# A transformer kernel of two blocks: the order of TensorE's instructions chosen from 80 plans, and 16 additions moved from GpSimd to VectorE

## The chip, the core and the metric

One core of a Trainium2 chip runs the kernel in one launch. The metric is the device time of one execution in microseconds (us). Three runs of the kernel before gave 2123.08, 2125.76 and 2126.22 us, median 2125.76 us.

In the profile PE is TensorE (matmuls and transposes), PEld its weight loads, ACT is ScalarE, DVE is VectorE, POOL is GpSimd and SP is SyncE, which issues the DMAs.

## What is computed

Two small transformers follow each other on one sequence of 256 tokens with 1024 channels, each two layers deep. All is fp32.

```python
def first_block(x, mem, ...):                      # two layers
        y = hybrid_mixer(x, ...)                   # three attentions, 8 heads of 64, gated and added
        x = layer_norm(alpha * x + y, ...)
        y = memory_cross_attention(x, mem, ...)    # 4 heads of 128
        x = layer_norm(alpha * x + y, ...)
        y = swiglu_ffn(x, w_gu, w_down)            # hidden width 2816
        x = layer_norm(alpha * x + y, ...)

def second_block(x, c, ...):                       # two layers
        h = _rmsnorm(x) * (1.0 + sc1) + sh1        # sc, sh, g come from c @ w_mod
        x = x + HALF_STEP * g1 * _swiglu(h, ...)
        h = _rmsnorm(x) * (1.0 + sc2) + sh2
        x = x + g2 * _hybrid_mixer(h, ...)         # stick-breaking, dilated, HGRN2; 4 heads each
        h = _rmsnorm(x) * (1.0 + sc3) + sh3
        x = x + HALF_STEP * g3 * _swiglu(h, ...)
```

In the first block's mixer the three branches are merged as `sum over n of sigmoid(gate_n) * (branch_n @ w_branch[n])`.

## The kernel before

**Tiling.** The 256 tokens are two halves of 128, and each half is a thread t = 0 or 1 with tiles of its own. A weight matrix comes in chunks of 128x1024 (tile `raw`). ScalarE rounds a chunk to fp32r (tile `wh`, or `E`), VectorE subtracts to get the rest (`wl`, or `E`), and both threads use the pair. The activations are split in the same way into two `S` tiles. A product is then three fp32r matmuls (`mm3`: high by high, low by high, high by low), each with 512 columns as a rule, added up in PSUM. A wide product gathers in `m` (one bank a thread), everything else in `a` (three banks a thread). Attention scores, the products of the probabilities with the values, and all transposes are plain fp32 matmuls of 128 columns in `a`. A plain fp32 matmul that is no transpose stands in the trace as two MATMUL records.

**Two forms of TensorE.** In `values` the heads are 64 wide, so the output has 64 partitions and the instruction uses half of the array's columns (tile size 128x64, in a row of the trace `128*64`, in the order `64x128`). Every other matmul uses the whole array (128x128). There are 192 matmuls of the first kind: 384 records. Below, a *visit* is an unbroken run of 64-wide matmuls between two whole-array instructions.

**What sets the order.** The program doesn't emit its instructions at once. A `Recorder` collects them with their tiles and dependencies, `plan` puts them in an order, and `emit` issues them in that order, all engines' queues at once. `listed` is a list scheduler. It keeps for each engine the instructions whose operands are ready by its own table of costs (`cost`), and takes the one with the earliest deadline `late`. The deadlines come from TensorE's instructions in the order in which the program recorded them: each is due when the slots before it are used up, and what it depends on is due earlier by its duration times `SLACK`. With `ROUNDS = 1` there is one plan. A change between the two forms of TensorE costs nothing in it.

**Around the moved work.** `branch` multiplies a product by its gate on VectorE and adds it to `merged` (tile `X`) on GpSimd for the second and third branch: 2 halves by 2 branches by 2 threads by 2 layers, 16 additions of 128x512. `transposed(merged, 8)` reads the sums on TensorE. `modulated` opens each of the second block's six parts in each thread, 12 times in all: two sums of squares from ScalarE are added with an epsilon by two small GpSimd instructions, a third takes the power -1/2 (`pow`), and VectorE scales `x` by it for eight transposes.

All instructions carry one line number in the profile, that of `emit`; tile names tell them apart.

Of the kernel before, what the change touches and what calls it, by code (L numbers as in the profile page):

```python
# [10 lines left out]
F32R = mybir.dt.float32r  # L11
U8 = mybir.dt.uint8
AF = mybir.ActivationFunctionType
ALU = mybir.AluOpType
# [7 lines left out]
RMS_EPS = 1e-6  # L22
# [107 lines left out]
TABLE = 1300  # L130
SLACK = 1.5
ROUNDS = 1
TRACE = 0
# [5 lines left out]
class Op:  # L139
    __slots__ = ("i", "eng", "name", "call", "args", "kw", "dur", "slot", "deps", "succ", "tiles", "set", "late", "start",  # L140
                 "wait", "ready", "nbytes")
# [6 lines left out]
class Recorder:  # L148
# [43 lines left out]
    def add(self, engine, name, args, kw):  # L192
        op = Op()
# [7 lines left out]
        for ap, write in [(a, False) for a in src] + [(a, True) for a in out]:  # L201
            n = ap.tensor.name
# [24 lines left out]
    def cost(self, op, name, out, src, kw):  # L227
        n = 1
        for step, k in list(out.ap)[1:]:
            n *= k  # L230
        wide = n
# [5 lines left out]
        if op.eng == "PE":  # L237
            return (4.7 + 0.4406 * n, 0) if src[1].dtype == F32R else ((1 if name == "transpose" else 2) * FP32, 0)
        if op.eng == "SP":
# [5 lines left out]
        if op.eng == "POOL":  # L245
            if name == "memset":
                return 200 + wide, 0
            return (400 if n == 1 else 700 + 2 * wide), 0
        acc = 83 if kw.get("accum_out") is not None else 0
# [13 lines left out]
    def plan(self):  # L263
        best, line = None, [op for op in self.ops if op.eng == "PE"]
        for op in self.ops:
            op.succ = []
        for op in self.ops:
            for d in op.deps:
                self.ops[d].succ.append(op.i)
        for _ in range(ROUNDS):  # L270
            order, time = self.listed(line)
            if best is None or time < best[1]:
                best = order, time, self.preload, [op.start for op in self.ops], {n: t.slot for n, t in self.tiles.items()}
            line = [op for op in order if op.eng == "PE"]
# [7 lines left out]
    def listed(self, line):  # L282

        import heapq
        ops = self.ops
# [13 lines left out]
        total = 0  # L299
        for op in line:  # L300
            op.late = total
            total += op.slot
        for op in reversed(ops):
# [9 lines left out]
            for j in reuse.get(op.i, ()):  # L313
                if ops[j].i > op.i and ops[j].late - dur < op.late:
                    op.late = ops[j].late - dur

        engines = ("PE", "ACT", "DVE", "POOL", "SP")
        ready = {e: [] for e in engines}
# [23 lines left out]
        dma, table, order, busy = 0.0, None, [], {e: False for e in engines}  # L342
        parked, later, progress = {}, [], 0.0

# [28 lines left out]
        while events:  # L373
# [18 lines left out]
            while again:  # L392
                again = False
                for e in engines:
                    if free[e] > now:
                        continue
                    q, held = ready[e], []
                    op = None
                    while q:
                        k = heapq.heappop(q)  # L400
                        if not room(k[2]):
                            continue
                        if e == "ACT" and k[2].set and table != k[2].set:
                            held.append(k)
                            if len(held) < 12:
                                continue
                            break
                        op = k[2]
                        break
                    if held and (op is None or held[0][0] + TABLE < op.late):  # L410
                        if op is not None:
# [21 lines left out]
                    free[e] = now + op.slot  # L433
                    push(free[e], 2, e)
                    end = now + op.dur
                    if e == "SP":
# [19 lines left out]
                    for j in op.succ:  # L456
                        s = ops[j]
                        v = (now + op.slot if e == "PE" else end) if s.eng == e != "SP" else end + NEXT[e][s.eng]
# [70 lines left out]
class Program:  # L529
# [173 lines left out]
    def modulated(self, x, sc, sh):  # L703
# [222 lines left out]
    def mixer(self, l, t, xT):  # L926
# [673 lines left out]
```

## Time and profile before

| | before |
|---|---|
| median of three runs | 2125.76 us |
| the profiled execution's own time | 2126.53 us |
| its span (first to last instruction) | 2124.5 us |
| TensorE busy | 2087.4 us (98%) |
| VectorE busy | 1567.6 us (74%) |
| ScalarE busy | 1214.4 us (57%) |
| GpSimd busy | 91.0 us (4%) |
| granted TensorE clock | 1.00 |

The chain of waits that ended last consists of TensorE nearly alone. A busy TensorE in this profile is not a TensorE at its peak: a record lasts longer than the step to the next one, since matmuls are pipelined, so the price of an instruction is read from start to start.

### The profile page before, as it was taken

Reading aid. Unit: us, or ns where it says so; the run is one execution under the profiler, and the core shown is the slowest. Engines: PE = TensorE matmul, PEld = TensorE weight load, DVE = VectorE, ACT = ScalarE, POOL = GpSimd, SP = SyncE. Lnnn points to the kernel's source line nnn. Section 1 sums busy time; section 2 is a strip of 40 time slices with the busy share of each in tenths; the row PEclk is TensorE's granted clock in tenths of the full one; section 3 lists DMA queues with packets and bytes.
Section 4 is the critical chain, followed back from the end, with each engine's and each line's share of the span. In section 5 each row is a group of like instructions: output and inputs, shape, how many; then the busy total and the mean of one; then the engine's idle time right before and its main releaser. Section 6 shows DMA issues by size and latency. Waiting matters only on the chain. (4 is left out here: it accounts for less than half of the span.)

```text
span 2124.5 us, 30068 instructions
## 1 busy us (share of the span) xinstructions
PE 2087.4 (98%) x10246; PEld 1690.9 (80%) x10246; DVE 1567.6 (74%) x3245; ACT 1214.4 (57%) x2538; POOL 91.0 (4%) x120
## 2 busy tenths in 40 slices
PE   8999999999999999999999999999999999999998
PEld 7788777888788878788878878878888887887887
DVE  5787888667888888877786678975566556997554
ACT  6977555444676755544454457764455445775442
POOL 0000200000000020000000000000000000000000
PEclk9999999999999999999999999999999999999999
DMA  7576776777767677688677652566656555256653
GB/s 265 162 251 217 245 252 218 253 253 257 250 218 256 215 253 256 214 265 267 227 243 246 234 182 96 160 189 189 192 176 188 171 187 185 71 162 204 187 185 105
DMA packets 150321, 443.20 MB, mean 209 GB/s; under 512 B 19208, under 2 KB 24344, under 8 KB 150168
## 3 DMA queue, kind: packets, MB, share of 16 engines
q1 hardware_dynamic: 150168, 441.29, 64.1%
q8 instruction: 80, 1.31, 0.2%
q14 instruction: 73, 0.60, 0.1%
HBM read 440.10 MB, written 1.12 MB: 208 GB/s over the span
## 5 line engine op out<-in xcount | busy, mean ns | idle before, releaser
L490 PE MATMUL m<-wh,S 128*128 128x512 f32 (+1 forms) x2944 | 932.0, 396 | 13.7 <-DVE S L490 4.6
L490 DVE TENSOR_TENSOR wl<-raw,wh 128x512 fp32r<-128x512 f32 (+1 forms) x982 | 652.4, 694 | 299.7 <-ACT wh L490 295.5
L490 ACT CAST wh<-raw 128x512 fp32r<-128x512 f32 (+1 forms) x982 | 563.9, 616 | 404.9 <-PE m L490 161.8
L490 PEld LDWEIGHTS m<-wh,S 128*128 128x128 f32 x2944 | 536.1, 188 | 137.4 <-DVE S L490 16.7
L490 PE MATMUL m<-wl,S 128*128 128x512 f32 (+1 forms) x1472 | 570.8, 392 | 0.0
L490 PE MATMUL m<-E,S 128*128 128x512 f32 x1308 | 346.0, 397 | 0.2
L490 PEld LDWEIGHTS m<-wl,S 128*128 128x128 f32 x1472 | 276.7, 188 | 56.8 <-issue 1.7
L490 PE MATMUL a<-wh,S 128*128 128x512 f32 x944 | 307.4, 399 | 3.8 <-ACT S L490 2.0
L490 DVE TENSOR_TENSOR E<-raw,E 128x512 fp32r<-128x512 f32 x334 | 218.5, 686 | 104.2 <-ACT E L490 84.7
L490 PEld LDWEIGHTS m<-E,S 128*128 128x128 f32 x1308 | 242.8, 188 | 53.7 <-DVE E L490 0.6
L490 ACT CAST E<-raw 128x512 fp32r<-128x512 f32 x334 | 192.8, 619 | 148.3 <-PE m L490 68.1
L490 PEld LDWEIGHTS a<-wh,S 128*128 128x128 f32 x944 | 173.2, 188 | 41.8 <-DVE S L490 3.7
L490 DVE SCALAR_TENSOR_TENSOR mr<-mr,c 128x512 f32<-128x512 f32 x288 | 192.7, 683 | 10.8 <-DMA mr<-in_w_mod 10.4
L490 PE MATMUL a<-E,S 128*128 128x512 f32 x648 | 184.7, 398 | 0.0
L490 PE MATMUL a<-wl,S 128*128 128x512 f32 x472 | 184.7, 394 | 0.0
L490 ACT CAST S<-a 128x256 fp32r<-128x256 f32 (+1 forms) x200 | 85.8, 429 | 126.2 <-PE a L490 125.0
L490 PEld LDWEIGHTS a<-E,S 128*128 128x128 f32 x648 | 119.7, 188 | 26.1 <-DVE E L490 0.6
L490 DVE TENSOR_TENSOR S<-a,S 128x256 fp32r<-128x256 f32 (+1 forms) x200 | 96.9, 490 | 46.0 <-ACT S L490 45.9
L490 PE MATMUL a<-c,T 128*128 128x128 f32 x652 | 120.8, 274 | 3.3 <-DVE T L490 2.4
L490 PEld LDWEIGHTS a<-c,T 128*128 128x128 f32 x652 | 84.7, 140 | 35.5 <-DVE T L490 6.3
L490 PEld LDWEIGHTS a<-wl,S 128*128 128x128 f32 x472 | 88.6, 188 | 19.3
L490 ACT ACTIVATE T<-m 128x256 f32<-128x256 f32 (+1 forms) x136 | 52.9, 389 | 78.8 <-PE m L490 78.4
(121 smaller groups left out, 1522.1 us busy)
## 6 DMA issues: line engine op xcount, KB each, us to landing
raw<-in_w_gu SPq DMA_DIRECT2D x264, 512.0 KB, 4.1
mr<-in_w_mod SPq DMA_DIRECT2D x288, 256.0 KB, 4.1
raw<-in_w_dn SPq DMA_DIRECT2D x132, 512.0 KB, 4.1
raw<-in_w_main SPq DMA_DIRECT2D x96, 512.0 KB, 4.1
raw<-in_w_in SPq DMA_DIRECT2D x56, 512.0 KB, 3.6
raw<-in_w_branch SPq DMA_DIRECT2D x24, 512.0 KB, 3.9
raw<-in_w_mo SPq DMA_DIRECT2D x16, 512.0 KB, 4.1
raw<-in_w_xkv SPq DMA_DIRECT2D x16, 512.0 KB, 4.2
```

The lines of the kernel that those rows point to most:

```text
L490: ins = op.call(*args, **{a: real(v, op) for a, v in op.kw.items()})
```

## The change

`plan` now computes the deadlines once and then makes 81 plans. It keeps the best by its own time. After a plan that is better it notes where TensorE waits for over 150 ns, and for each such wait the chain of instructions that led to it (`chain`). For the next trial one to eight of these chains get deadlines that are earlier by 0.5 to 9 us, or later by 1 us; a trial that is no better is undone. The table of costs changes too: `listed` charges a change of TensorE's form (`ENTER`, `LEAVE`), and it stays in the form it is in while an instruction of that form is ready and not due much later than the first one of another form (`STAY`: 12 us for the whole array, 25 us for the 64-wide form). `SLACK` goes from 1.5 to 1.7. In the kernel's arithmetic, the 16 additions go from GpSimd to VectorE, and in `modulated` one VectorE instruction takes the place of the two small GpSimd additions.

```diff
-SLACK = 1.5
-ROUNDS = 1
+STAY = 12000, 25000
+ENTER, LEAVE = 130, 250
+SLACK = 1.7
+SEARCH = 80
...
+        op.mode = 0
+        if op.eng == "PE" and src[1].dtype != F32R:
+            op.mode = 1 if out[0].ap[0][1] == 64 else 2 if src[0].ap[0][1] == 64 else 0
...
+        for n in range(SEARCH + 1):
+            order, time = self.listed()
             if best is None or time < best[1]:
...
+                chains = [(w, self.chain(op)) for w, op in waits]
...
+            else:
+                for op, b in trial.items():
+                    op.late += b
...
+            size = (500, 1500, 4000, 9000, -1000)[(seed >> 8) % 5]
+            for _ in range((1, 1, 2, 4, 8)[(seed >> 16) % 5]):
+                seed = seed * 1103515245 + 12345 & 0x7fffffff
+                for op in chains[(seed >> 8) % len(chains)][1]:
+                    trial[op] = size
+            for op, b in trial.items():
+                op.late -= b
...
+                        if e == "PE" and k[2].mode != mode:
+                            if not aside:
+                                limit = k[0] + STAY[mode > 0]
+                            elif k[0] > limit:
+                                aside.append(k)
+                                break
+                            aside.append(k)
+                            continue
...
+                    if e == "PE" and op.mode != mode:
+                        start = now + (LEAVE if mode else 0) + (ENTER if op.mode else 0)
+                        mode = op.mode
...
-        nc.gpsimd.tensor_scalar(m, ms[:, 0:1], RMS_EPS, None, op0=ALU.add)
-        nc.gpsimd.tensor_tensor(m, m, ms[:, 1:2], op=ALU.add)
+        nc.vector.tensor_scalar(m, ms[:, 0:1], ms[:, 1:2], RMS_EPS, op0=ALU.add, op1=ALU.add)
...
-                    nc.gpsimd.tensor_tensor(m, m, gs[h], op=ALU.add)
+                    nc.vector.tensor_tensor(m, m, gs[h], op=ALU.add)
```

The built programs have the same 9632 matmuls and transposes, the same ScalarE work but for 50 activation table loads instead of 46, and the same DMAs. VectorE has 28 instructions more, GpSimd 40 fewer. The 192 matmuls of the 64-wide form stand in 56 visits before (44 of four matmuls, 2 of three, 10 of one), and in 24 after (6 of four, 12 of eight, 6 of twelve).

Three places show it. The first is TensorE in layer 0, thread 1, where the 64-wide matmuls add to `a_155` the products of the probabilities `T` with the values `S`; the `m` tiles are wide products of the mixer. Before:

```order
L490 MATMUL a_155_751<-T_215_1001,S_108_494 64x128
L490 MATMUL m_213_998<-wl_885,S_6_168 128x256
L490 MATMUL m_194_948<-wh_820,S_25_234 128x424
L490 MATMUL m_213_998<-wh_907,S_9_193 128x256
L490 MATMUL a_155_751<-T_215_1001,S_108_494 64x128
L490 MATMUL m_213_998<-wh_907,S_10_202 128x256
L490 MATMUL m_194_948<-wh_820,S_26_240 128x424
L490 MATMUL m_213_998<-wl_919,S_9_193 128x256
L490 MATMUL a_155_751<-T_215_1001,S_127_604 64x128
```

After, at the same products:

```order
L558 MATMUL m_194_956<-wl_854,S_25_233 128x424
L558 MATMUL a_155_758<-T_199_954,S_108_494 64x128 x2
L558 MATMUL a_155_758<-T_199_954,S_127_598 64x128 x2
L558 MATMUL a_155_758<-T_215_1019,S_108_494 64x128 x2
L558 MATMUL a_155_758<-T_215_1019,S_127_598 64x128 x2
L558 MATMUL m_232_1081<-wh_973,S_161_777 128x512
```

The four single matmuls of `T_215`, each a visit of its own, and the four of `T_199` from further up now stand in one visit of eight.

The second place is TensorE at the end of layer 0's cross-attention. `a_711` is thread 1's attention output; ScalarE and VectorE split it into `S_755` and `S_756` for the output projection in `a_757` and `a_758`. `a_746` and `a_747` are the same projection of thread 0. Before:

```order
L490 MATMUL a_747_3642<-E_3453,S_745_3636 128x512
L490 MATMUL a_747_3642<-E_3467,S_744_3627 128x512
L490 MATMUL a_711_3625<-T_754_3633,S_738_3581 128x128
L490 MATMUL a_711_3625<-T_754_3633,S_739_3567 128x128
L490 MATMUL a_757_3704<-wh_3348,S_755_3700 128x512
L490 MATMUL a_758_3707<-wh_3348,S_755_3700 128x512
L490 MATMUL a_757_3704<-wh_3348,S_756_3709 128x512
```

After, first the end of `a_711` and the start of thread 0's projection, and then the start of thread 1's:

```order
L558 MATMUL a_711_3614<-T_754_3600,S_738_3576 128x128
L558 MATMUL a_711_3614<-T_754_3600,S_739_3552 128x128
L558 MATMUL a_746_3636<-wh_3313,S_744_3621 128x512
L558 MATMUL a_747_3638<-wh_3313,S_744_3621 128x512
L558 MATMUL a_746_3636<-wh_3313,S_745_3630 128x512
...
L558 MATMUL a_747_3638<-E_3429,S_745_3630 128x512
L558 MATMUL a_747_3638<-E_3445,S_744_3621 128x512
L558 MATMUL a_757_3689<-wh_3313,S_755_3642 128x512
L558 MATMUL a_757_3689<-wh_3313,S_756_3650 128x512
```

The 24 matmuls of thread 0's projection, which stood ahead of the last `a_711`, now stand between it and its use.

The third place is VectorE at the last additions of layer 0's third branch: `S_585` is the gated product, `X_28` the merged sum, `wl` the low parts of weights, `S_610` the low part of the transposed sum's first half. Before, when the addition is GpSimd's:

```order
L490 TENSOR_TENSOR S_585_2839<-m_601_2891,S_585_2839 128x512
L490 TENSOR_TENSOR wl_2944<-raw_2875,wh_2934 128x512 x2
L490 TENSOR_TENSOR S_610_2954<-a_608_2936,S_609_2948 128x512
L490 TENSOR_TENSOR wl_2969<-raw_2900,wh_2960 128x512 x2
L490 TENSOR_TENSOR S_613_2980<-a_611_2962,S_612_2973 128x512
```

After:

```order
L558 TENSOR_TENSOR S_585_2817<-m_601_2885,S_585_2817 128x512
L558 TENSOR_TENSOR wl_2923<-raw_2862,wh_2911 128x512
L558 TENSOR_TENSOR X_28_1269<-X_28_1269,S_585_2817 128x512
L558 TENSOR_TENSOR S_610_2935<-a_608_2921,S_609_2929 128x512
L558 TENSOR_TENSOR wl_2923<-raw_2862,wh_2911 128x512
```

The addition stands in VectorE's queue, one half-chunk of a weight behind the gated product.

## Rows read from the trace of the kernel before

**Rows 1.** Page, busy time: us, share of the span, instructions.

```profile
PE 2087.4 (98%) x10246; PEld 1690.9 (80%) x10246; DVE 1567.6 (74%) x3245; ACT 1214.4 (57%) x2538; POOL 91.0 (4%) x120
```

**Rows 2.** Timeline, PE, seven waits: start, us, instruction [idle before <-releaser].

```profile
338.20 0.73 PE L490 MATMUL a<-wh,S 128*128 128x512 f32 x2 [0.68 <-ACT S L490]
339.82 0.50 PE L490 MATMUL a<-wh,S 128*128 128x512 f32 x1 [0.88 <-DVE S L490]
354.03 0.50 PE L490 MATMUL m<-wh,S 128*128 128x512 f32 x1 [1.82 <-DVE T L490]
880.60 0.50 PE L490 MATMUL m<-wh,S 128*128 128x512 f32 x1 [1.68 <-DVE T L490]
1063.93 0.50 PE L490 MATMUL m<-wh,S 128*128 128x512 f32 x1 [0.70 <-DVE S L490]
1347.60 0.73 PE L490 MATMUL m<-wh,S 128*128 128x512 f32 x2 [0.68 <-ACT S L490]
1399.52 0.66 PE L490 MATMUL a<-c,X 128*128 128x128 f32 x4 [1.09 <-DVE X L490]
```

**Rows 3.** Timeline, PE, a visit of four 64-wide matmuls.

```profile
135.72 0.39 PE L490 MATMUL m<-wh,S 128*128 128x512 f32 x1
136.04 0.66 PE L490 MATMUL a<-T,S 128*64 128x128 f32 x8
136.63 0.50 PE L490 MATMUL m<-wh,S 128*128 128x512 f32 x1
136.97 0.40 PE L490 MATMUL m<-wl,S 128*128 128x512 f32 x1
```

**Rows 4.** Chain of waits, two pieces: start, us, what; 512-column matmuls, then whole-array fp32.

```profile
1833.94 1.17 PE m L490 x5
1835.11 0.89 PE a L490 x8
```

**Rows 5.** Timeline, PE, a visit of one matmul between 256-column ones.

```profile
90.52 0.39 PE L490 MATMUL m<-wh,S 128*128 128x256 f32 x2
90.85 0.43 PE L490 MATMUL a<-T,S 128*64 128x128 f32 x2
91.21 0.39 PE L490 MATMUL m<-wl,S 128*128 128x256 f32 x1
91.43 0.47 PE L490 MATMUL m<-wh,S 128*128 128x424 f32 x2
```

**Rows 6.** Timeline, all engines, around the addition of the third branch.

```profile
264.92 2.37 DVE L490 TENSOR_TENSOR wl<-raw,wh 128x512 fp32r<-128x512 f32 x2
265.14 1.60 POOL L490 TENSOR_TENSOR X<-X,S 128x512 f32<-128x512 f32 x1 [4.33 <-DVE S L490]
266.80 0.66 PE L490 MATMUL a<-c,X 128*128 128x128 f32 x4 [0.52 <-POOL X L490]
267.81 1.28 DVE L490 TENSOR_TENSOR wl<-raw,wh 128x512 fp32r<-128x512 f32 x2
```

**Rows 7.** Timeline, DVE and PE, layer norm of layer 1's cross-attention, then its transposes.

```profile
865.03 0.67 DVE L490 SCALAR_TENSOR_TENSOR X<-X,a 128x512 f32<-128x512 f32 x1
869.97 0.66 PE L490 MATMUL a<-c,X 128*128 128x128 f32 x4
```

**Rows 8.** Timeline, ACT and POOL, the small instructions of one `modulated`.

```profile
1397.30 0.18 ACT L490 ACTIVATION_READ_ACCUMULATOR X<-X 128x1 f32 x1
1397.90 0.58 POOL L490 TENSOR_TENSOR s<-s,c 128x1 f32<-128x1 f32 x1
```

**Rows 9.** Group by line: xcount, busy us, mean ns, idle us before.

```profile
L490 DVE TENSOR_SCALAR s<-s 128x1 f32<-128x1 f32 (+2 forms) x40 | 6.0, 153 | 0.1
```

**Rows 10.** Timeline, ACT, a table load and what follows it.

```profile
1807.47 1.28 ACT L486 ACT_TABLE_LOAD   x1
1808.77 0.63 ACT L490 ACTIVATE T<-T 128x512 f32<-128x512 f32 x1
```

**Rows 11.** A stretch: us, busy us (count) of each engine, granted clock, DMA share, GB/s.

```profile
1300.00:1400.00 100.00, 98.03 (x569) 80.35 (x570) 93.81 (x218) 70.31 (x161) 7.94 (x8) 1.00 0.43 134
```

More of the change, by code (lines that the diff above doesn't have):

```diff
@@ L139 @@
 class Op:
-    __slots__ = ("i", "eng", "name", "call", "args", "kw", "dur", "slot", "deps", "succ", "tiles", "set", "late", "start",
+    __slots__ = ("i", "eng", "name", "call", "args", "kw", "dur", "slot", "deps", "succ", "tiles", "set", "mode", "late", "boost", "start",
                  "wait", "ready", "nbytes")
@@ L247, in cost @@
                 return 200 + wide, 0
-            return (400 if n == 1 else 700 + 2 * wide), 0
+            return (600 if n < 8 else 700 + 2 * wide), 0
         acc = 83 if kw.get("accum_out") is not None else 0
@@ L263, in plan @@
     def plan(self):
-        best, line = None, [op for op in self.ops if op.eng == "PE"]
         for op in self.ops:
-            op.succ = []
+            op.succ, op.boost = [], 0.0
         for op in self.ops:
@@ L269, in plan @@
                 self.ops[d].succ.append(op.i)
-        for _ in range(ROUNDS):
-            order, time = self.listed(line)
+        self.deadlines()
+        best, seed, trial = None, 1, {}
+        for n in range(SEARCH + 1):
+            order, time = self.listed()
             if best is None or time < best[1]:
-                best = order, time, self.preload, [op.start for op in self.ops], {n: t.slot for n, t in self.tiles.items()}
-            line = [op for op in order if op.eng == "PE"]
+                best = order, time, self.preload, [op.start for op in self.ops], {k: t.slot for k, t in self.tiles.items()}
+                waits, stop = [], 0.0
+                for op in order:
+                    if op.eng == "PE":
+                        if op.start > stop + 150 and op.start > 15000:
+                            waits.append((op.start - stop, op))
+                        stop = op.start + op.slot
+                chains = [(w, self.chain(op)) for w, op in waits]
+                if TRACE:
+                    print(n, time)
+            else:
+                for op, b in trial.items():
+                    op.late += b
+            trial = {}
+            if not chains:
+                break
+            seed = seed * 1103515245 + 12345 & 0x7fffffff
+            size = (500, 1500, 4000, 9000, -1000)[(seed >> 8) % 5]
+            for _ in range((1, 1, 2, 4, 8)[(seed >> 16) % 5]):
+                seed = seed * 1103515245 + 12345 & 0x7fffffff
+                for op in chains[(seed >> 8) % len(chains)][1]:
+                    trial[op] = size
+            for op, b in trial.items():
+                op.late -= b
         self.preload = best[2]
@@ L280, in plan, with chain, deadlines @@
         return best[:2]
-    def listed(self, line):
-        import heapq
+    def chain(self, op):
+        out, until = [op], op.start - 14000
+        while op.deps:
+            op = max((self.ops[d] for d in op.deps), key=lambda d: d.start + d.dur)
+            if op.start < until:
+                break
+            out.append(op)
+        return out
+    def deadlines(self):
         ops = self.ops
@@ L299, in listed @@
         total = 0
-        for op in line:
-            op.late = total
-            total += op.slot
+        for op in ops:
+            if op.eng == "PE":
+                op.late = total
+                total += op.slot
         for op in reversed(ops):
@@ L342, in listed @@
         dma, table, order, busy = 0.0, None, [], {e: False for e in engines}
-        parked, later, progress = {}, [], 0.0
+        parked, later, progress, mode, idle = {}, [], 0.0, 0, 0.0
         def safe(s, t, taken):
@@ L407, in listed @@
                             break
+                        if e == "PE" and k[2].mode != mode:
[3 more added lines that the diff above has]
+                                aside.append(k)
+                                break
+                            aside.append(k)
+                            continue
+                        if e == "PE" and aside and k[0] > limit:
+                            aside.append(k)
+                            break
                         op = k[2]
                         break
+                    if aside:
+                        if op is None:
+                            aside.sort()
+                            op = aside.pop(0)[2]
+                        for k in aside:
+                            heapq.heappush(q, k)
                     if held and (op is None or held[0][0] + TABLE < op.late):
@@ L432, in listed @@
                             heapq.heappush(ready["SP"], (x.late, x.i, x))
-                    free[e] = now + op.slot
+                    start = now
+                    if e == "PE" and op.mode != mode:
+                        start = now + (LEAVE if mode else 0) + (ENTER if op.mode else 0)
+                        mode = op.mode
+                    free[e] = start + op.slot
+                    if e == "PE":
+                        if now > idle + 30 and op.dur > 150:
+                            free[e] += 100
+                        idle = free[e]
                     push(free[e], 2, e)
-                    end = now + op.dur
+                    end = start + op.dur
                     if e == "SP":
@@ L457, in listed @@
                         s = ops[j]
-                        v = (now + op.slot if e == "PE" else end) if s.eng == e != "SP" else end + NEXT[e][s.eng]
+                        v = (start + op.slot if e == "PE" else end) if s.eng == e != "SP" else end + NEXT[e][s.eng]
                         s.ready = max(s.ready, v)
```

7 lines of the change are left out of this document (5 added, 2 removed).

## The prediction, made before the changed kernel ran

> **What bounds the kernel now.** I read the page's busy times first. TensorE is busy for 2087.4 of 2124.5 us [rows 1]; the other engines leave a quarter of the span or more. So the time falls in two ways only: TensorE's 37.1 us of idle time shrink, or the same matmuls cost less. Next I read the waits of PE. Behind the first DMA they are short and many, on tiles that ScalarE or VectorE have just written. The long ones are in [rows 2], and in each the reader is to see what came late: the two parts of a split attention output at 338.20 and 339.82, a PSUM tile `m` whose reader is late at 354.03 and 880.60. None is a wait for a weight, so the DMA queue is not the limit. Last I read the timeline of PE from start to start, since busy time hides lost time, and there the 64-wide matmuls stand out.
>
> **Part one: fewer visits to the 64-wide form.** In [rows 3] a 512-column matmul starts at 135.72, and the second one behind the visit at 136.97: 1.25 us for two 512-column matmuls and four 64-wide ones. The next one starts 0.23 us behind a 512-column matmul where nothing is between (1.17 us for five in a run [rows 4]). Here it is 0.32 behind the one at 135.72 and 0.34 behind the one at 136.63: 0.09 and 0.11 us are lost in plain sight at the visit's two edges. 1.25 less 0.46 is 0.79 us for the visit. What would its four matmuls cost without a change of form? Eight whole-array fp32 records take 0.89 us [rows 4], 0.11 each. The two records of a 64-wide matmul lie on top of each other, so four such steps are 0.44 us. The visit itself costs 0.35 us.
>
> The small visit gives the other end. From 90.52 to 91.43 [rows 5] three 256-column matmuls (0.12 us each, half of the 0.23) and one 64-wide take 0.91 us. 0.55 us remain, 0.44 above the step of 0.11. So the price hangs on the visit and little on what is in it: 0.55 us with one matmul, 0.79 with four.
>
> The order has 56 visits before and 24 after, so 32 go. At 0.35 us that is 11.2 us, at 0.44 it is 14.1. If only the plain edges (0.09 and 0.11) went with a visit, and the rest stayed with each group of four, it would be 6.4 us. I take 11.2, since 44 of the 56 visits have the size of [rows 3].
>
> **Part two: TensorE's waits.** For each wait I counted the matmuls that the order puts between the last one that the late tile depends on and the one that waits.
> - 338.20 and 339.82, 0.68 + 0.88 us: none before, 24 now, 5.5 us of work at 0.23 for a chain that was 1.6 us late. Both go.
> - Four more waits of 0.67 to 0.68 us (at 545, 1348, 1851 and 1874 us; the second is in [rows 2]) have the form of the first. None between before; now 13, 33, 3 and 33. Together 2.7 us, of which I leave 0.2.
> - 880.60, 1.68 us: 4 before, 13 now. 354.03, 1.82 us: 2 before, 10 now, most of them short transposes of 0.11; I leave 0.9.
> - 1063.93, 0.70 us, and one of 0.36 just behind it, together 1.06: 10 before, 14 now. 1399.52, 1.09 us: 28 before, 36 now.
> - Two transposes that wait 0.52 us each for a GpSimd addition ([rows 6] and its double in layer 1): part three. With what I leave of the last three lines, 0.5 us.
>
> That is 0.68 + 0.88 + 2.7 + 1.68 + 1.82 + 1.06 + 1.09 + 1.04 = 10.95 us, of which 1.6 stay. New waits: in layer 1's cross-attention thread 0's projection now starts three transposes (0.33 us) behind its attention output, the pattern of 338.20 and 339.82 that costs 1.56 us without cover; I take 1.0. And the transposes of its layer norm now stand 13 matmuls behind the last projection matmul (eight fp32 of 0.22 and five of 0.23, 2.9 us), while the chain between took from 865.03 to 869.97 [rows 7], 4.9 us. A wait of about 1.1 us lies in between anyhow, and VectorE did other work in that time, so I take 0.5 (0 to 0.9). Net: 10.95 - 1.6 - 1.5 = 7.8 us.
>
> The same counts show what the change can't reach: the waits at 235, 763, 867, 1074 and 1792 us keep their distance and stay.
>
> **Part three: GpSimd's work on VectorE.** Sixteen additions at 0.64 us (half of the pair at 267.81) look like 10 us more for VectorE. [Rows 6] shows otherwise: the two weight casts at 264.92 take 2.37 us beside GpSimd's addition of 1.60, the two at 267.81 take 1.28. The addition holds VectorE up for 1.09 us, longer than doing it would. Ten of the sixteen stretch a cast like that, so about 11 us of stretch go and 10 us of work come: VectorE's load stays where it was. The chain gets shorter: 1.60 us become 0.64 ahead of the transposes that waited 0.52 us, though 13 matmuls stand there now instead of 17. What hides an addition on VectorE is its place: it waits for its own engine alone, and the half chunk of `wl` behind it is wanted microseconds later. Without that cover it costs its 0.64 us, at all sixteen 10 us.
>
> In `modulated` the second sum of squares is there at 1397.48 and `pow` starts at 1397.90 [rows 8]. These 0.42 us become one VectorE instruction of 0.15 [rows 9] and the hops to and from it: a gain of 0.2 us when VectorE is free, a loss of up to 0.5 when it has just begun a cast of 0.64. TensorE waits behind two of these twelve chains. I count nothing, with bounds of -2.4 and +6 us over all twelve.
>
> Four table loads come on top, on a ScalarE that is busy for 57%. In [rows 10] a load takes 1.28 us and the next instruction starts 0.02 us behind it. I count nothing, and 5.2 us if TensorE stood behind each. The Trainium skill ("ScalarE: Activation LUTs", What ACT_TABLE_LOAD costs) puts a change of set at 1283 ns and another 1380 ns of drain, 2.66 us in all. The trace agrees with the first figure and shows no drain; by the Trainium skill's total four loads would hold ScalarE for an estimated 10.6 us, and the sum would still not move unless TensorE waited for them.
>
> **The sum.** 2126.53 (this execution's own time: a span of 2124.5 and 2.0 us around it) - 11.2 - 7.8 = 2107.5; I say 2107 us. This execution lies 0.8 us above the median of the three runs.
>
> **The rivals.**
> - *The visits go, the waits move.* The planner meets its chains elsewhere, with VectorE at 94% in the densest stretch [rows 11]. For it: many of today's short waits are not on chains that are too short by count, but on instructions that queued behind a cast. Against it: the long ones had next to nothing between, and now have. 2126.5 - 11.2 = 2115 us.
> - *More than that.* A visit is worth its 0.44 us, and small waits that hide under the overlap of two records go too, another 2 us: 2126.5 - 14.1 - 9.8 = 2103.
> - *The price of the form goes with each group, not with the visit.* Then moving groups together gives nothing, and the waits alone count: 2126.5 - 7.8 = 2119. Against it: [rows 3, 5], a quarter of the matmuls at 70% of the price.
> - *Slower: a plan picked for its thin margins.* The best of 81 plans by the planner's own table is one in which operands arrive just in time by that table. In the attention stretches, where VectorE is 94% busy [rows 11], an operand that queues behind one half-chunk cast comes 0.64 us late, and TensorE, which takes its instructions in order, stops with it. From 30 such new waits on the 19 us are gone; with 40 it is 2107 + 26 = 2133 us. For it: the wait at 235 us, with 6 matmuls between, is of that kind. Against it: before, such waits are a dozen, and the groups of 64-wide matmuls, which had 4 to 8 matmuls ahead of them in most cases, now have 12 and more in most.
>
> **How the numbers follow.** Forecast 0.55 (its own range 2103 to 2112, from what may stay at 354.03, the new waits and `modulated`), the waits move 0.23, more 0.10, the price goes with the group 0.06, slower 0.06. The range reaches from the larger gain to the price per group, with a margin for the bounds on the visit: 2099 to 2120. About 0.2% (4.3 us) is what a measurement of this kernel can tell from no change. Faster, below 2121.5: the first four but a tail of the second and fourth, 0.88. Within 0.2%: that tail and the mildest of the slower case, 0.07. Slower: 0.05.
>
> **What would show it.** In the profile after, TensorE's busy time should be about 11 us lower (near 2076) and its idle time 7 to 8 us (near 29). The edges of [rows 3] should appear 24 times, and a visit of eight should take about 1.23 us. Of the waits of [rows 2] only a rest at 354.03 should be left; two new ones of about 1 and 0.5 us should stand in layer 1's cross-attention. No weight cast on VectorE should be stretched beyond 0.7 us. The forecast is wrong if TensorE's busy time stays at 2087 (price per group), if its idle time stays at 37 (the waits moved) or grows past 55 (thin margins).

## The result, and the profile after

| | before | after |
|---|---|---|
| median of five runs | 2126.22 us (2123.08 to 2127.01) | 2103.04 us (2099.30 to 2107.26) |
| the profiled execution's own time, its span | 2126.53, 2124.5 us | 2107.26, 2105.5 us |
| TensorE busy, idle | 2087.4, 37.1 us | 2076.8, 28.7 us |
| mean granted clock, profiled run | 1.000 | 0.995 |

The ratio of after to before is 0.9895, with a 95% interval of 0.9878 to 0.9912: 23 us faster. The forecast was 2107 us with a range of 2099 to 2120; the forecast's own range was 2103 to 2112. The sum was made for the profiled execution, and that one took 2107.26 us, where 2107.5 stood. It looks like a sum that came out to the digit. It isn't, as the rest of this section shows: terms that I had not counted cancel.

The busy times, page of after (us, share of the span, instructions), to be held against [rows 1]:

```profile
PE 2076.8 (99%) x10246; PEld 1700.5 (81%) x10246; DVE 1568.0 (74%) x3273; ACT 1215.7 (58%) x2542; POOL 55.1 (3%) x80
```

A visit of eight 64-wide matmuls in after (timeline of PE: start, us, instruction), the counterpart of [rows 3]:

```profile
189.00 0.63 PE L558 MATMUL m<-wh,S 128*128 128x512 f32 x2
189.47 0.39 PE L558 MATMUL m<-wl,S 128*128 128x512 f32 x1
189.79 1.09 PE L558 MATMUL a<-T,S 128*64 128x128 f32 x16
190.82 0.50 PE L558 MATMUL m<-wh,S 128*128 128x512 f32 x1
191.16 0.39 PE L558 MATMUL m<-wl,S 128*128 128x512 f32 x1
```

From 189.47 to 191.16 are 1.69 us; less two 512-column steps (0.46) this is 1.23 us, what the prediction said for eight. The visits of four in [rows 3] take 0.79 us, those of twelve 1.66: 0.35 for the visit and 0.11 for each matmul.

The waits of TensorE in after that are longer than 0.6 us from 40 us on (timeline of PE, the wait and what ended it in brackets); before has 18 of them, seven of which stand in [rows 2]:

```profile
56.47 0.73 PE L558 MATMUL m<-wh,S 128*128 128x512 f32 x2 [1.57 <-ACT S L558]
59.47 1.09 PE L558 MATMUL a<-c,T 128*128 128x128 f32 x4 [1.58 <-DVE T L558]
...
349.66 0.52 PE L558 MATMUL a<-c,X 128*128 128x128 f32 x3 [1.41 <-DVE X L558]
...
851.58 0.50 PE L558 MATMUL a<-wh,S 128*128 128x512 f32 x1 [0.68 <-ACT S L558]
854.20 0.79 PE L558 MATMUL a<-wh,S 128*128 128x512 f32 x1 [1.88 <-DVE S L558]
1061.50 0.77 PE L558 MATMUL m<-wh,S 128*128 128x512 f32 x1 [2.22 <-DVE T L558]
1255.18 0.50 PE L558 MATMUL m<-wh,S 128*128 128x512 f32 x1 [0.69 <-ACT T L558]
1777.16 0.50 PE L558 MATMUL m<-wh,S 128*128 128x512 f32 x1 [0.69 <-ACT T L558]
```

All seven of [rows 2] are gone. The two at 56 and 59 us stand where before has two of the same kind, of 0.26 and 0.31 us (at 52.41 and 55.51); the pair at 851 and 854 and the one at 1061 stood in before too, with 0.68, 0.42 and 0.99 us, and have grown.

What the prediction does not speak of stands in the sixth column of the windows of after (from:to us, length, busy us of PE, PEld, DVE, ACT and POOL with counts, then the granted clock):

```profile
52.00:58.00 6.00, 4.33 (x19) 2.89 (x17) 5.42 (x27) 5.98 (x14) 0.00 (x0) 1.00 0.72 277
58.00:65.00 7.00, 5.53 (x20) 4.94 (x21) 5.07 (x14) 4.38 (x14) 0.00 (x0) 0.51 0.26 77
65.00:72.00 7.00, 7.00 (x40) 5.80 (x38) 5.75 (x10) 6.09 (x13) 0.00 (x0) 1.00 0.46 138
846.00:853.30 7.30, 5.64 (x32) 4.48 (x30) 6.44 (x14) 2.85 (x5) 0.00 (x0) 1.00 0.56 194
853.30:860.20 6.90, 6.00 (x18) 5.03 (x19) 5.36 (x10) 1.17 (x2) 0.57 (x1) 0.51 0.23 77
860.20:866.00 5.80, 5.80 (x26) 4.71 (x26) 2.52 (x6) 2.42 (x3) 0.00 (x0) 1.00 0.58 183
1061.50:1065.00 3.50, 3.50 (x9) 2.80 (x10) 3.50 (x6) 2.43 (x7) 0.20 (x1) 0.51 0.35 125
```

Three times in this execution TensorE's clock falls to its lower level, 1.2 GHz: for 6.83 us from 58.04, for 6.83 from 853.35 and for 3.41 from 1061.56, in or just behind the longest waits. In the profile of before it does not fall until the end.

The wait of 2.22 us has a DMA behind it. TensorE's `m` comes free when VectorE has read it for `T`. Ahead of that stands an activation of ScalarE, and ahead of this in ScalarE's queue two casts of a weight that had waited 1.54 us for their DMA (timeline of ACT and DVE):

```profile
1059.57 1.14 ACT L558 CAST E<-raw 128x512 fp32r<-128x512 f32 x2 [1.54 <-DMA raw<-in_w_gu]
1060.62 0.37 ACT L558 ACTIVATE T<-m 128x256 f32<-128x256 f32 x1
1061.02 0.42 DVE L558 TENSOR_TENSOR T<-T,m 128x256 f32<-128x256 f32 x1
```

The five runs of after line up by their mean clock: 0.995 took 2107.26 us, 0.998 took 2105.67 and 2103.04, 0.999 took 2101.90, and 1.000 took 2099.30. The kernel before is not free of this, but loses less: its 37 timed runs of the experiments below lie at 0.998 (7 runs, mean 2127.6 us), 0.999 (21, 2126.8) and 1.000 (9, 2126.0). A mean of 0.999 is no proof of a fall within the run: the profiles of `one_load` and `best` below have it with the low stretch at the end alone.

**Where the 19 us between the two profiles are.** I summed TensorE's time from start to start, from the first matmul to the last, in both profiles. From the two steps on either side of each visit I took what its matmuls need without it (0.23 us for 512 columns, 0.11 for a whole-array record or a 64-wide matmul): that is the row of visits. The last row is what remains when the unhindered steps, the visits, the idle time that the profile shows and the slow clock are taken off. It is mostly the hidden part of each wait: the record of a 512-column matmul lasts 0.39 us, but the next one could start 0.23 us behind it [rows 4], so that TensorE has been waiting for 0.16 us when the profile begins to call it idle. Behind the first matmul the profile of before has 67 such waits (idle of any length), that of after 33, and 34 x 0.16 is 5.4 us. In the other columns the counts come within 1.2 us of the row in the same way; that the row is the hidden part is worked out from them, and no run was made for it.

| us | before | additions only | first plan only | after | waits filled |
|---|---|---|---|---|---|
| first to last matmul | 2113.2 | 2108.2 | 2092.6 | 2093.8 | 2086.3 |
| visits | 20.7 | 20.9 | 8.3 | 8.1 | 8.1 |
| idle shown | 26.1 | 23.6 | 21.3 | 17.4 | 11.5 |
| at 1.2 GHz, beyond full clock | 0 | 0 | 1.7 | 7.5 | 0 |
| waits shown, count | 67 | 53 | 43 | 33 | 33 |
| the rest: what waits cost beyond their idle time | 26.6 | 24.0 | 21.6 | 21.1 | 20.1 |

(The unhindered steps are 2039.7 us in each; in the last column 6.9 us of extra matmuls come on top. The three columns between are explained below; the last row has no true zero, only its differences count.) From before to after: visits -12.6, idle -8.7, the hidden part of the waits -5.5, slow clock +7.5, together -19.3 us.

### The profile page after: what moved, and what is told of

The parts are those of the page before. It is cut to its first block, busy times and chain, and to the rows that moved or that the text cites. A ratio compares the mean times of both kernels' runs of the same rounds, so it can differ in the third digit from the quotient of the medians.

```text
span 2105.5 us, 30023 instructions
## 1 busy us (share of the span) xinstructions
PE 2076.8 (99%) x10246; PEld 1700.5 (81%) x10246; DVE 1568.0 (74%) x3273; ACT 1215.7 (58%) x2542; POOL 55.1 (3%) x80
## 5 line engine op out<-in xcount | busy, mean ns | idle before, releaser
L558 DVE TENSOR_TENSOR wl<-raw,wh 128x512 fp32r<-128x512 f32 (+1 forms) x982 | 640.7, 683 | 285.1 <-ACT wh L558 281.3
L558 PE MATMUL m<-wl,S 128*128 128x512 f32 (+2 forms) x1472 | 571.4, 393 | 0.0
```

The source lines that it names most:

```text
L558: ins = op.call(*args, **{a: real(v, op) for a, v in op.kw.items()})
```

## Experiments

Each kernel was timed against the kernel before on the same chip, whose median in the three sets was 2126.49, 2127.39 and 2126.61 us. "The changed kernel" is the one described above.

**1. The additions alone** (`part_three`). The kernel before with two edits:

```diff
-        nc.gpsimd.tensor_scalar(m, ms[:, 0:1], RMS_EPS, None, op0=ALU.add)
-        nc.gpsimd.tensor_tensor(m, m, ms[:, 1:2], op=ALU.add)
+        nc.vector.tensor_scalar(m, ms[:, 0:1], ms[:, 1:2], RMS_EPS, op0=ALU.add, op1=ALU.add)
...
-                    nc.gpsimd.tensor_tensor(m, m, gs[h], op=ALU.add)
+                    nc.vector.tensor_tensor(m, m, gs[h], op=ALU.add)
```

> The kernel before with part three alone: the sixteen additions in branch and the sum in modulated go to VectorE; one plan, mode changes not counted, 56 visits. Theory (the stretch of the casts that goes pays for the additions): VectorE's busy time within 5 us of the 1584 us before, no weight cast over 0.72 us beside a GpSimd addition, the two waits of 0.52 us gone, time 2122 to 2126 us, that is 0 to 3 us off. Rival (the additions hold VectorE up): VectorE's busy time 10 us higher, TensorE's idle time above 40 us, time 2129 us or more.

(The 1584 us in it was a slip: VectorE's busy time before is 1567.6 [rows 1].) Measured: 2124.13 us, ratio 0.9987 (0.9978 to 0.9996), 2.4 us faster. The page's busy times, and the weight casts (columns: count, minimum, median and maximum in ns, first and last start):

```profile
PE 2085.0 (98%) x10246; PEld 1691.2 (80%) x10246; DVE 1568.3 (74%) x3273; ACT 1214.1 (57%) x2538; POOL 57.8 (3%) x80
...
L490 DVE TENSOR_TENSOR wl<-raw,wh x982: 541/684/750, 5.1 to 2089.5; 128x512 fp32r<-128x512 f32 x191, 128x424 fp32r<-128x424 f32 x3, 128x384 fp32r<-128x384 f32 x3
```

VectorE does 28 instructions more and is busy for 0.7 us more; its slowest cast takes 0.75 us, where [rows 6] showed a pair of 2.37. The two waits of 0.52 us for a GpSimd sum are gone. The stretch does pay for the additions. The Trainium skill ("GPSIMD Engine Reference", 1. Specifications) says that GpSimd and VectorE share an SBUF interface and collide where a VectorE instruction has two SBUF inputs; the cast `wl<-raw,wh` has two, and with GpSimd's 128x512 additions gone its stretch is gone, so the traces agree. By the table the gain lies in the waits: 14 fewer, 2.5 us of idle time and 2.6 us of their hidden part. These 5.1 us are those of one execution, which at 2121.24 us was the fastest of eleven; the medians show 2.4.

**2. One plan instead of 81** (`one_plan`): the changed kernel with `SEARCH = 0`.

> The changed kernel with SEARCH = 0: its planner counts the changes of tile mode and the additions are on VectorE, but only the first plan is made. The plan has 24 visits to the 64-wide form, as the changed kernel's, and by the planner's table its waits are about 3 us longer. Theory (visits and waits are two separate gains, and the 80 trials bring only the last part of the waits): TensorE busy 2077 us as in the changed kernel, idle 32 to 35 us, time 2105 to 2109 us. Rival (the trials bring all that the waits lost): busy 2077 us, idle 37 us as before, time 2113 to 2116 us.

Measured: 2105.19 us (2104.20 to 2109.49), ratio 0.9901 (0.9888 to 0.9915). Time and idle time (32.5 us) are the theory's. TensorE's busy time is 2071.7 us and not 2077: the changed kernel's 2076.8, from which the 2077 was taken, has three slow stretches in it, and this profile one, of 3.41 us behind a wait of 2.35 at 1058.15. By the table the first plan already has nearly all: the visits, and 21.6 against 21.1 us in the last row. The 80 trials take 3.9 us of shown idle away. In the medians 2.2 us are left of that, and the intervals of the two ratios overlap: that the trials gain time is not shown. The changed kernel loses more to its clock (7.5 against 1.7 us in the table). This run has the new `SLACK` and the new table of costs too, so it does not say what these two do to the waits.

**3. The trials without the modes** (`no_modes`):

```diff
-            op.mode = 1 if out[0].ap[0][1] == 64 else 2 if src[0].ap[0][1] == 64 else 0
+            op.mode = 0
```

> The changed kernel, its planner told that no matmul has a tile mode (op.mode = 0): 80 trials and the additions on VectorE stay, the 64-wide matmuls are no longer held together. 54 visits instead of 24. By the planner's own table its waits are as long in sum as the changed kernel's. Theory (0.36 us for a visit, and the trials bring the same): the changed kernel at full clock takes 2099.5 us, 30 visits more make 10.8, so 2109 to 2112 us, TensorE's busy time 2077 to 2081 us at full clock (the changed kernel's is 2068.3, worked out from the run with the filled waits: 2075.2 less 6.9). Rival (free of the modes the trials shorten the waits by another 5 us): 2105 us. Rival (the price hangs on the matmuls): 2100 us.

Measured: 2112.22 us, ratio 0.9930 (0.9918 to 0.9942), just above the theory's range. The median run has a granted clock of 1.000, as has the changed kernel's run of 2099.30: 12.9 us between them. Of these the visits outside the profile's one slow stretch make 11.5 us: with each step counted once, 53 of them take 19.6 us, where the changed kernel's 24 take 8.1. So holding the visits together is what moves this kernel most, and the two rivals are out.

**4. Visits split on purpose** (`split`). The changed kernel's own order; `pad` issues matmuls that nobody reads, into a PSUM tile that is free at that place:

```diff
+        for a, b in zip(line, line[1:]):
+            run = run + 1 if a.mode == 1 else 0
+            if run and run % 4 == 0 and b.mode == 1:
+                out[a.i] = 1
...
+        for k in range(count):
+            ins = src.call(tile, lhsT, rhs, start=True, stop=True)
...
+                    if op.i in fill:
+                        self.pad(tc, op, fill[op.i], n, last_use, recent, spot)
```

> The changed kernel in its own order, with one 512-column matmul that nobody reads put behind a group of four 64-wide matmuls wherever another group follows in the same visit, at 22 of 24 such places: 46 visits instead of 24, the same number of 64-wide matmuls. Theory (0.35 us for each visit): 22 x (0.35 + 0.23) = 12.8 us more busy time on TensorE, 2089 us, and 2114 to 2117 us in all. Rival (the price goes with each group of four): 22 x 0.23 = 5.1 us more, 2107 to 2109 us.

Measured: 2114.60 us (2114.23 to 2116.41), ratio 0.9943 (0.9931 to 0.9956). A visit of twelve, split into three (timeline of PE):

```profile
68.32 0.63 PE L590 MATMUL m<-wh,S 128*128 128x512 f32 x2
68.87 0.66 PE L590 MATMUL a<-T,S 128*64 128x128 f32 x8
69.46 0.50 PE L556 MATMUL pad<-wh,S 128*128 128x512 f32 x1
69.89 0.66 PE L590 MATMUL a<-T,S 128*64 128x128 f32 x8
70.48 0.49 PE L556 MATMUL pad<-wh,S 128*128 128x512 f32 x1
70.91 0.66 PE L590 MATMUL a<-T,S 128*64 128x128 f32 x8
71.49 0.51 PE L590 MATMUL m<-wl,S 128*128 128x512 f32 x1
```

From one group to the next are 1.02 us: four 64-wide matmuls (0.44), the whole-array one between (0.23), and 0.35 for the visit. It is 0.34 to 0.35 at 20 of the 22 places. At the other two, at 189.68 and 710.71 us, it is 0.57: there the weight load of the second group waits for a `T` of ScalarE (PEld is the weight load):

```profile
190.30 0.45 PEld L590 LDWEIGHTS a<-T,S 128*64 128x64 f32 x8 [0.44 <-ACT T L590]
```

The price goes with the visit, not with the group of four. TensorE's busy time is 2084.2 us and not 2089, since the 2089 was built on the changed kernel's 2076.8 with its slow stretches.

**5. The waits filled** (`fill`). Again the changed kernel's own order; the numbers name the instruction of TensorE ahead of each wait:

```diff
+        return {393: 6, 407: 6, 6543: 2, 6648: 7, 8132: 9}
```

> The changed kernel in its own order, with 30 more 512-column matmuls that nobody reads, put at the ends of five waits of TensorE: 6 and 6 in those of 1.57 and 1.58 us at 56 and 59 us, 2 and 7 in those of 0.68 and 1.88 us at 851 and 854 us, 9 in that of 2.22 us at 1061 us. TensorE works through the waits, and what it waits for comes no earlier. Theory (the stretches at 1.2 GHz behind these three places come from these waits): granted clock 1.000 in every run, PE busy 2076.8 - 8.5 (the slow stretches of 17 us at half cost) + 6.9 (30 at 0.23 us) = 2075, idle 22, time 2098 to 2100 us in all runs. Rival (the falls come from elsewhere): clock 0.995 to 1.000 and times from 2099 to 2107 us as in the runs of the changed kernel.

Measured: 2100.02 us, the four runs from 2099.32 to 2100.53, ratio 0.9873 (0.9859 to 0.9886), mean clock 1.000, 0.999, 1.000 and 1.000: two runs lie up to 0.5 us above the theory's 2098 to 2100, and the rival's 2107 us and 0.995 do not come up. Its page, and windows around the three places (columns as above):

```profile
PE 2075.2 (99%) x10276; PEld 1698.5 (81%) x10276; DVE 1566.8 (75%) x3273; ACT 1215.6 (58%) x2542; POOL 55.2 (3%) x80
...
50.00:64.00 14.00, 13.88 (x73) 11.20 (x73) 13.32 (x44) 12.62 (x30) 0.00 (x0) 1.00 0.64 219
846.00:860.00 14.00, 13.79 (x73) 11.29 (x72) 11.19 (x22) 5.13 (x8) 0.60 (x1) 1.00 0.49 149
1050.00:1064.00 14.00, 13.90 (x66) 10.78 (x65) 13.75 (x31) 8.85 (x21) 1.10 (x2) 1.00 0.70 223
```

TensorE does 30 matmuls more, is busy for 1.6 us less, and the clock stays up at all three places. Without the 6.9 us of its idle matmuls TensorE would be busy for 2068.3 us: this is what the changed kernel's order needs at full clock.

**6. Two of the five filled** (`fill_two`): as 5, with `return {393: 6, 407: 6}`.

> As the run with the filled waits, but only the first two are filled (6 matmuls each at 56 and 59 us); those at 851, 854 and 1061 us are left empty, as in the changed kernel. Theory (a fall of the clock belongs to the wait at its place): the clock stays at 1.00 until 850 us and falls near 854 or 1061 us or at both, in most runs; mean clock 0.998 to 1.000, time 2099 to 2102 us, 0 to 2.6 us above the run with all five filled. Rival (a first fall early in the run brings the later ones): no fall at all, 2099.5 to 2100.5 us and clock 1.000.

Measured: 2101.02 us (2097.88 to 2101.89), clocks 1.000, 0.998, 1.000 and 1.000. The profiled execution has no fall before the end, though these two waits stand in it:

```profile
851.63 0.50 PE L584 MATMUL a<-wh,S 128*128 128x512 f32 x1 [1.26 <-DVE S L584]
...
1055.86 0.50 PE L584 MATMUL m<-wh,S 128*128 128x512 f32 x1 [1.83 <-DVE T L584]
```

The theory's "in most runs" is not borne out: the waits are shorter here than in the changed kernel's profile (1.88 and 2.22), and one run of four shows a lower clock. Whether a first fall makes the later ones likelier, this does not settle. Nor does the length of a wait settle whether the clock falls. The profile of run 4 has the same two waits as this one, 0.68 and then 1.26 us:

```profile
862.33 0.50 PE L590 MATMUL a<-wh,S 128*128 128x512 f32 x1 [1.26 <-DVE S L590]
...
862.70:866.10 3.40, 3.40 (x14) 2.90 (x13) 2.85 (x6) 1.17 (x2) 0.00 (x0) 0.50 0.13 17
```

There the clock fell, for 3.41 us from 862.70; here it stayed up.

**7. Waits made on purpose** (`halts`). The run 5, and at three places where TensorE was never idle:

```diff
+        self.halts = {3499: 2, 8923: 2, 12995: 2}
...
+            for _ in range(5 if op.i in self.halts and not k else 0):
+                self.nc.vector.tensor_copy(tile, tile)
```

> The run with the five filled waits, and three new waits made on purpose, at 455, 1160 and 1690 us of the changed kernel, where TensorE is busy all the time and the granted clock is 1.00: a matmul that nobody reads, five copies of its PSUM tile onto itself on VectorE, and another such matmul, which has to wait for them. TensorE should wait some 3.5 to 4.5 us at each (five VectorE instructions of about 0.69 us, the hops to and from them, and what VectorE has in its queue). Theory (a long wait of TensorE brings the clock down where it stands): the granted clock falls to 0.5 in or just behind each of the three, for 3.4 to 6.8 us, and at none of the five filled places; time 2100 + 3 x 4.0 + 3 x 1.7 to 3.4 = 2117 to 2122 us. Rival (the falls have to do with the places in the changed kernel, not with the waits): the clock stays at 1.00 at all three, 2111 to 2114 us.

Measured: 2120.48 us (2119.45 to 2123.61, ten runs), ratio 0.9972 (0.9962 to 0.9981). The three waits, and the windows at them:

```profile
458.23 0.65 PE L551 MATMUL pad<-wl,S 128*128 128x512 f32 x1 [4.53 <-DVE pad L553]
...
1165.94 0.80 PE L551 MATMUL pad<-E,S 128*128 128x512 f32 x1 [3.73 <-DVE pad L553]
...
1702.43 0.80 PE L551 MATMUL pad<-wl,S 128*128 128x512 f32 x1 [3.73 <-DVE pad L553]
...
450.00:458.40 8.40, 3.87 (x17) 2.81 (x17) 7.41 (x14) 2.18 (x4) 0.00 (x0) 1.00 0.83 266
458.40:461.80 3.40, 3.40 (x9) 2.63 (x10) 1.67 (x4) 1.14 (x2) 0.00 (x0) 0.50 0.22 78
461.80:465.00 3.20, 3.20 (x15) 2.59 (x14) 0.77 (x2) 1.14 (x2) 0.00 (x0) 0.99 0.58 164
1165.00:1171.80 6.80, 5.86 (x15) 4.60 (x16) 4.32 (x10) 0.77 (x2) 0.00 (x0) 0.50 0.52 152
1700.80:1707.70 6.90, 5.26 (x12) 4.13 (x13) 3.72 (x7) 0.59 (x2) 0.00 (x0) 0.51 0.23 76
```

The clock falls three times in this execution, for 3.41, 6.83 and 6.83 us, in or just behind each of the three waits, and nowhere else until the end. In a slow stretch a 512-column matmul starts 0.43 us behind the one before it, not 0.23 (three in 1.28 us here):

```profile
1166.53 1.48 PE L587 MATMUL a<-E,S 128*128 128x512 f32 x3
1167.81 1.05 PE L587 MATMUL a<-wh,S 128*128 128x512 f32 x2
```

The profiled execution took 2123.61 us, the longest of the ten, 24.3 more than that of run 5. The three waits are 12.0 of that; TensorE is busy for 14.5 us of the slow stretches, which at 0.20 of each 0.43 costs 6.7; the six matmuls more are 1.4. Of the other 4.2 us, 2.4 are idle time elsewhere; the rest was not followed. All ten runs have a mean clock of 0.996 or 0.997, those of run 5 0.999 or 1.000. Together with 5 this shows the cause: a long wait of TensorE can bring the clock down where it stands, and three of 3.7 to 4.5 us each did so in this profile. What VectorE does in these waits is to copy a tile in PSUM, with no DMA.

**8. The table loads** (`one_load`). The planner of the changed kernel places 49 loads of ScalarE's tables (one more of the 50 stands outside its order), and 8 of them bring a table of which nothing is issued before the next load. At 52.87 us two follow each other for 2.57 us, shortly ahead of the wait of 1.57. One rule more for the planner:

```diff
+                    if e == "ACT" and owed is not None and owed.wait == 0 and room(owed):
+                        op, owed = owed, None
...
+                        owed = held[0][2]
```

> The changed kernel with one rule more in its planner: once a table of ScalarE is loaded, the operation that it was loaded for is issued first. The order of the changed kernel has 49 loads, 8 of them with no operation of their set before the next load; this one has 43 and none of these. Theory (the wait of 1.57 us at 56 us, behind two loads of 2.57 us in a row, and that of 1.58 behind it come from a wasted load): both are gone or under 0.5 us each, the clock doesn't fall there, ScalarE's busy time 1215.7 - 7.7 = 1208 us, time 2097 to 2101 us. Rival (they come from VectorE's small instructions of the position table, which run at the same time): the waits stay, 2101 to 2105 us.

Measured: 2101.01 us (2100.07 to 2103.32), ratio 0.9879 (0.9866 to 0.9893); ScalarE is busy for 1209.5 us. The place of the two waits:

```profile
55.25 0.72 PE L563 MATMUL m<-wh,S 128*128 128x512 f32 x2 [1.28 <-ACT S L563]
...
57.85 0.63 PE L563 MATMUL a<-c,T 128*128 128x128 f32 x4 [0.48 <-DVE T L563]
```

Half a miss: the second wait is short now, the first is still 1.28 us, with one load and a 1.06 us ScalarE instruction in front of it. The clock stays up there. As a version it is no better than 5.

**9. All of it together** (`best`): the rule of 8, `SEARCH = 300`, and matmuls put into every wait over 0.8 us that the plan itself foresees.

> The rule for the table loads, 300 trials instead of 80, and a filler: wherever the plan itself leaves TensorE idle for over 0.8 us, 512-column matmuls that nobody reads are put into the wait, as many as fit with 0.3 us to spare (7 places). By the planner's table 1.5 us less than the changed kernel. Theory (waits of TensorE cost their own length, and where they come close to each other the clock as well): granted clock 1.000 in every run, 2096 to 2099 us, below the run with the filled waits (2100.0). Rival (the planner's last microseconds are not on the chip): 2100 us, as with the filled waits alone. Rival (the extra matmuls run into the end of their waits): 2103 us or more.

Measured: 2100.58 us (2099.93 to 2102.51), ratio 0.9877 (0.9864 to 0.9891), mean clock 0.999, 0.998, 1.000 and 0.999, not 1.000 in every run. Waits of 1.71 and 1.54 us still stand in the profile, at 55.61 and 337.02. The theory missed, and it is the first rival that came: the microseconds that the planner's table still promises are not there on the chip. Against the changed kernel (0.9895, 0.9878 to 0.9912) neither this nor run 5 (0.9873, 0.9859 to 0.9886) is shown to be faster by the ratios alone; what run 5 shows is that its four runs lie within 1.2 us, at the lower edge of the changed kernel's 8 us.

## Why the prediction was right, step by step

**Visits: right, and 1.4 us short.** -11.2 was said, -12.6 came. The price of 0.35 us is that of the visits of four and holds: 0.34 on average after (8.1 for 24), 0.34 to 0.35 at most places of run 4. Those of one matmul cost 0.44 to 0.46 [rows 5], and all ten went, as did the two of three, which cost the same: 44 x 0.35 + 12 x 0.45 = 20.8 us before, the 20.7 of the table. I had seen that price and used one for all.

**Waits of TensorE: the sum right, the places half.** -7.8 was said, and idle time went from 37.1 to 28.7, -8.4 (-8.7 behind the first matmul). All of [rows 2] went, as counted. At 354.03 I left a rest of 0.9; that wait is gone, and another chain waits 1.41 us at 349.66. Of the two new waits one came, with 0.35 us at 843.08 instead of 1.0, the other didn't. I said that the waits at 867 and 1074 us stay: they grew to 1.88 and 2.22 us, and those at 235 and 763, said to stay, are gone. The waits that the prediction lists changed by -9.1 us in all, those that it does not name by +0.5: the longest of these to go had 1.21 us, at 1266.85, while those at 56 and 59 us grew to 1.57 and 1.58 and the 1.41 came. That the parts cancel so nearly is luck. The rows of VectorE ahead of the one at 854.20 show how a count of matmuls misses this (timeline of DVE):

```profile
852.07 0.75 DVE L558 SCALAR_TENSOR_TENSOR X<-X,s,row 128x512 f32<-128x512 f32 x1
852.74 0.15 DVE L558 TENSOR_SCALAR s<-s 128x1 f32<-128x1 f32 x1
852.80 0.74 DVE L558 SCALAR_TENSOR_TENSOR X<-X,s,row 128x512 f32<-128x512 f32 x1
853.46 0.68 DVE L558 TENSOR_TENSOR S<-a,S 128x512 fp32r<-128x512 f32 x1
```

The `S` that TensorE waits for is ready to be made when ScalarE's part is, before 851.58. It queues behind two instructions of the other thread's layer norm, and comes 1.5 us later for it. This is the mechanism of the slower rival, at one place instead of thirty.

**GpSimd's additions on VectorE: right.** VectorE's load stays where it was, no cast is stretched (0.75 us is the longest, 0.70 among those of 512 columns), and the two waits go. The prediction counted ten stretched casts and 11 us; the trace of before has 14 casts of 512 columns over 0.8 us, in all 12.6 us longer than at 0.64 each. That the four table loads cost nothing is not shown: two loads in a row stand ahead of the wait at 56.47, and without wasted loads this wait and the one behind it are 0.3 and 1.1 us shorter (run 8).

**Not in the sum: the hidden part of the waits, -5.5 us.** I priced a wait by the idle time that the profile shows, and a wait costs 0.16 us more than that. One rival had 2 us for small waits under the overlap of two records; that the overlap belongs to every wait, the shown ones too, I didn't see. 34 fewer waits make it 5.4 us. Among the gains this is the term that was mis-sized most: waits are worth 14.2 us in all, not 7.8.

**Not in the text at all: the clock, +7.5 us in the profiled run.** The prediction asked what each wait costs in length. It did not ask where two waits stand close together. In before, waits of 1.82 and 1.68 us had left the clock at 1.00 [rows 2], in a profile without a fall ahead of its end; the change made fewer waits, and some of them longer or nearer to each other, and its runs reach down to a mean clock of 0.995, those of before to 0.998. The test that I had set, a busy time "near 2076", was met by accident: 2068.3 by run 5, 7.5 of slow clock, and 1.0 that stays open. At full clock this order took 2099.3 us in its one such run, where the forecast's own range began at 2103 and the stated range at 2099.

## What to carry to other kernels

A change of TensorE's form has a price per visit, so collect the matmuls of one form; here that was the largest part, and the first plan that counted it had nearly all of the gain. Where a kernel's runs differ by more than those of its predecessor, put the granted clock beside each time before looking for another cause, and look at the longest waits. Idle time that can't be removed may be filled with matmuls that nobody reads: it gains nothing by itself, and here it held the clock (run 5).

## What the runs showed of the hardware

Waits of TensorE for ScalarE or VectorE bring its clock from 2.4 to 1.2 GHz, in stretches of 3.41 or 6.83 us in these profiles. It fell in or behind single waits of 2.22 (after), 2.35 (run 2), 3.73 and 4.53 us (run 7), and behind two in a row: 1.57 and 1.58, 0.68 and 1.88 (after), 1.49 and 1.57 (run 3), 0.68 and 1.26 us (run 4). Single waits of 1.82 (before), 1.83 (run 6) and 1.71 us (run 9) left it up, and so did two in a row of 0.68 and 1.26 us in run 6 and of 0.95 and 1.57 us in run 4. So the length of these waits alone does not tell whether it falls. The Trainium skill ("TensorE: Matmul & The Clock Gate", HAM oscillation — how this bites in real kernels) tells of the same loss behind waits for a DMA, with half of the slow time as its price. The traces come near to that price (0.43 us a step in place of 0.23, run 7), and the waits of run 7 show that it takes no DMA.

A visit to the 64-wide form costs 0.35 us between 512-column matmuls, with four, eight or twelve matmuls in it (0.79, 1.23 and 1.66 us), and the same when a single whole-array matmul stands between two visits (20 of 22 places of run 4). A visit of one matmul between narrower ones costs 0.44 to 0.46 [rows 5].
